# A hybrid attention/Fourier layer on eight cores: last token part of 128 with grouped scaling and stores, a fourth x slot, six rather than eight modulation blocks before attention and these later, head sums of squares on ScalarE, the second half of the first queries behind the Fourier part

## The chip, the cores and the metric

The kernel runs on all 8 cores of one Trainium2 chip. Each core works for itself: cores 2b and 2b+1 share batch entry b, each owns half of its 2048 tokens, computes keys and values for all of them, and does the queries, the output projection and the MLP for its own 1024. Nothing is exchanged between cores.

The time is the device time of the slowest core, in microseconds (us). A program on eight cores has a second, slower state in some executions: the cores of one die, or both, are granted a lower TensorE clock (in one execution of the kernel before four cores had 0.83 to 0.84 and the others 0.98, and it took 1936.8 us). Runs marked slow are left out everywhere; ratios use fast runs alone. "Clock" is the granted TensorE clock as a share of the full one.

Engines: PE is TensorE (PEld its weight loads), DVE is VectorE, ACT is ScalarE, POOL is GpSimd, SP is SyncE.

## The reference, cut to what matters

```python
h = modulate(rmsnorm(x, g1), sh1, sc1)
q, k, v, u = split_proj(h @ w_in)            # 12 query heads, 4 key/value heads, 4 Fourier groups
q = apply_axial_rope(rmsnorm(heads(q), q_g), tabs)
k = apply_axial_rope(rmsnorm(heads(k), k_g), tabs)
attn = latent_attention(q, k, v, kc, vc)     # over 256 context keys and 2048 latent keys
four = fourier_mix(u, w_f)
x = x + gt1 * (concat([attn, four]) @ w_out)
h2 = modulate(rmsnorm(x, g2), sh2, sc2)
x = x + gt2 * sq_relu_mlp(h2, w1, w2)
return rmsnorm(x, final_norm_g)
```

The six vectors `sh1 ... gt2` come from `silu(c) @ w_ada`. This matrix is read in 48 blocks of 1 MB (as bf16 on the chip). Blocks 8 to 15 (scale 1) are needed before the first projection, 0 to 7 (shift 1) soon after it, 16 to 47 only after attention.

## The kernel before: the parts that matter here

The program is first recorded as a list of operations with a priority ("level") each. A planner in the kernel file then orders the operations of every engine with a cost model, and adds the semaphore waits. Each operand is booked as one range of bytes:

```python
    def span(self, ap):                     # one range from the first to the last byte touched
        dims = list(ap.ap)
        row = dims[0][0]
        lo = hi = ap.offset % row
        ...
        return space, lo, hi
```

Loading x. Eighteen token tiles go through three slots of 8 KB per partition, from tile 6 on through two of them, because the third is reused for the "middle" modulation blocks (`wadm`, blocks 16 to 23):

```python
        ADM = [at('wadm', 160, [16, 256], BF16)]
        XS = [at('xs_%d' % i, 144 + 8 * i, [16, 128]) for i in range(3)]
        ...
            xi = n % 3 if n < 6 else n % 2
        ...
        first = [vu(n) for n in range(3)]            # three tiles before the first weights are complete
        ...
        for n in range(NLATE, 18):                   # NLATE = 7
            (some.pop(0) if some else vu(n))()()
            if n < NLATE + 5:
                chains[n - NLATE]()
            if n < NLATE + 8:
                ada(9 + n, ADM, 'adm', 1, 1, [4])    # eight blocks, from tile 7 on
```

Then the Fourier part, all eight tiles of the first four query heads (`q_block(0, ...)`), and attention, into which `side()` mixes the other query heads and modulation blocks 24 to 47.

The end. The last two blocks of the MLP are finished for tokens 0 to 511, then 512 to 767, then 768 to 1023. For each part and each of 16 row blocks: eight matmuls, a residual add on DVE, a square on ACT, a matmul with ones for the sum of squares; then the final norm:

```python
        for n, (tg, lo, hi) in enumerate(((0, 0, 512), (1, 0, 256), (1, 256, 512))):
            ...
            for d in range(16):
                a = ACC(tg, d)[:, lo:hi]
                if n == 2 and d % 3 == 1:
                    R.tt(a, a, rb, ALU.mult, eng='pool')
                else:
                    R.stt(a, a, fgc[:, d:d + 1], rp, ALU.mult, ALU.mult)
                R.dma('sp', rows(out_d, tg * 16 + d)[:, lo:hi], a, 'out%d' % (d % 4), load=False)
```

That is 48 stores, one for each row block and part.

Of the kernel before, what the change touches and what calls it, by code (L numbers as in the profile page):

```python
# [13 lines left out]
D = 2048  # L14
# [16 lines left out]
class Rec:  # L31
# [20 lines left out]
            a = a.rearrange("p (a b c) -> p a b c", a=shape[0], b=shape[1])  # L52
        return a

    def span(self, ap):
        dims = list(ap.ap)
        row = dims[0][0]
        lo = hi = ap.offset % row
        for step, n in dims[1:]:
            if step >= 0:  # L60
                hi += step * (n - 1)
            else:
                lo += step * (n - 1)
        es = 2 if ap.dtype == BF16 else 4
        space, b = self.base[ap.tensor.name]
        lo, hi = b + lo * es, b + (hi + 1) * es
        if space == 'P':
            lo, hi = lo // 2048 * 2048, -(-hi // 2048) * 2048
        return space, lo, hi


    def add(self, eng, fn, reads=(), writes=(), dur=0.1, dma=None, nbytes=0, level=None, after=()):
        r = [self.span(a) for a in reads]
        w = [self.span(a) for a in writes]
        i = len(self.ops)
        if dma is not None:
            self.dma_cnt[dma] = self.dma_cnt.get(dma, 0) + 16
            ev = ('d', dma, self.dma_cnt[dma])
        else:
            ev = ('c', eng, i)  # L80
        self.ops.append(dict(i=i, eng=eng, fn=fn, r=r, w=w, dur=dur, dma=dma, nbytes=nbytes, ev=ev, after=after,
                             prio=(self.level if level is None else level, i + self.lag)))
        return i
# [84 lines left out]
    def dma(self, q, out, in_, key, load=True, level=None, after=()):  # L168
        nb = 4 * 128 * (self.fs(out) if load else self.fs(in_))
        return self.add(q, lambda e: e.dma_start(out=out, in_=in_), [] if load else [in_], [out] if load else [],  # L170
                        0.55 if q == 'pool' else 0.06, dma=key, nbytes=nb, level=level, after=after)


    def graph(self):
# [228 lines left out]
KORDER = [ORDER[n] for n in (5, 6, 7, 0, 8, 1, 9, 2, 10, 3, 11, 4, 14, 15, 16, 17)]  # L403


CB = {}
CF = {}

# [17 lines left out]
def build_program():  # L426
# [25 lines left out]
    with ExitStack() as st:  # L452
# [58 lines left out]
        AD0 = [at('wada_%d' % i, 108 + 8 * i, [16, 256], BF16) for i in range(4)]  # L511
        ADM = [at('wadm', 160, [16, 256], BF16)]
        AD1 = [at('wadb_%d' % i, 144 + 8 * i, [16, 256], BF16) for i in range(3)]
        XS = [at('xs_%d' % i, 144 + 8 * i, [16, 128]) for i in range(3)]
        SQ = [at('sqx_%d' % i, 168 + 4 * i, [16, 128], BF16) for i in range(2)]
        Y = [at('y_%d' % i, 176 + 2 * i, [512]) for i in range(4)]
        YL = Y[0:1] + [at('yl_%d' % i, kb, [512]) for i, kb in enumerate((46, 54, 140, 142, 186, 190))]
# [112 lines left out]
        def evac(out, in_, which, n=2):  # L630
            R.copy(out, in_, 'act' if rot(which, n) == 0 else 'dve')

        def head_norm(y, slot):

            t2 = T2[slot]
            c = qst[:, rot('qst', 16), :]
            R.act(t2, y, AF.Square)
            R.add('dve', lambda e, a=c[:, 0:4], b=t2.rearrange("p (h d) -> p h d", h=4):
                  e.tensor_reduce(out=a, in_=b, axis=AX.X, op=ALU.add), [t2], [c[:, 0:4]], 0.6)
            R.act(c[:, 4:8], c[:, 0:4], AF.Ln, scale=1.0 / 128, bias=EPS)  # L640
            R.act(c[:, 8:12], c[:, 4:8], AF.Exp, scale=-0.5)
            return c[:, 8:12].unsqueeze(2).to_broadcast([128, 4, 128])
# [4 lines left out]
        def qk(bank, y, rstd, bias, rope, g2, dst, late=False, slot=None, on_act=False):  # L647
            if late:
                R.tt(y, y, bias, ALU.add)
            else:  # L650
                R.stt(y, PS[bank], rstd, bias, ALU.mult, ALU.add)
            s = rot('t12', 2) if slot is None else slot
            t1, t2, xb = T1[s], T2[s], XB[s]
            rh = head_norm(y, s)
            if rope is None:
                R.tt(h3(t1), h3(y), g2[:, 0:128].unsqueeze(1).to_broadcast([128, 4, 128]), ALU.mult)
            else:
                rog = ROG[rot('rope', 2)]
                four = lambda a: a.rearrange("p (c f n) -> p c f n", c=2, f=2)
                R.tt(four(rog), rope.rearrange("p (c n) -> p c n", c=2).unsqueeze(2).to_broadcast([128, 2, 2, 64]), four(g2), ALU.mult)  # L660
                cg, sg = rog[:, 0:128], rog[:, 128:256]
                R.tt(h3(t1), h3(y), cg.unsqueeze(1).to_broadcast([128, 4, 128]), ALU.mult)
                for f in range(2):
                    R.tt(h3(t2)[:, :, 64 * f:64 * f + 64], h3(y)[:, :, 64 - 64 * f:128 - 64 * f],
                         sg[:, 64 * f:64 * f + 64].unsqueeze(1).to_broadcast([128, 4, 64]), ALU.mult)
                R.tt(t1, t1, t2, ALU.add)
            if on_act:
                for i in range(4):
                    R.act(h3(xb)[:, i, :], h3(t1)[:, i, :], AF.Copy, scale=rh[:, i, 0:1])
            else:  # L670
                R.tt(h3(xb), h3(t1), rh, ALU.mult)
            return lambda tbank: qk_out(xb, dst, tbank)
# [10 lines left out]
        def vu(n):  # L683
            t = ORDER[n]
            R.level = 0.95
            r = 1 if t >= 16 else 0
            xi = n % 3 if n < 6 else n % 2
            x = XS[xi]
            R.dma('sp', x.rearrange("p k n -> p (k n)"), rows(xt_d, t), 'xs%d' % xi)
            sq = SQ[n % 2]  # L690
# [42 lines left out]
            def keys():  # L733
# [3 lines left out]
                if n < NLATE:  # L737
                    R.act(y, PS[b], AF.Copy, scale=rstd)

                def chain(slot=None):  # L740
                    R.level = 1
                    rope = None
                    if r == 0:
                        c = rot('ropek', 16)
                        assert ORDER[n] == KORDER[c]
                        rope = ROP[c // 2 % 2]
                        if c % 2 == 0:
                            R.dma('sp', rope.rearrange("p k n -> p (k n)"), rows(ropek_d, c // 2), 'rope%d' % (c // 2 % 2))
                        rope = rope[:, c % 2, :]
                    qk(b, y, rstd, BKC if r else BK, rope, kg2, kT[:, :, t * 128:(t + 1) * 128], n < NLATE, slot, True)(7 - rot('tb', 2))  # L750
                return chain
            return keys

        first = [vu(n) for n in range(3)]
        last = load_win(3, WK, 'wk', 0.1, last)
        for i in range(8):
            last = ada(i, AD0[0:2], 'adz', 0.2, 0.5, [7, 6], last)
# [5 lines left out]
        bias_bc(selb[0], 6, BV)  # L763
        bias_col(WU, 7, buc, cfv('dmask'))

        chains = [keys() for keys in first] + [vu(n)() for n in range(3, NLATE)]
        some = [vu(n) for n in range(NLATE, 10)]
        for n in (5, 6):
            chains[n](0)
        for n in range(NLATE, 18):  # L770
            if n >= 15:
                some += [vu(i) for i in range(15, 18) if n == 15]
            (some.pop(0) if some else vu(n))()()
            if n < NLATE + 5:
                chains[n - NLATE]()
            if n < NLATE + 8:
                ada(9 + n, ADM, 'adm', 1, 1, [4])


        def q_block(cbk, pbanks, tbanks):  # L780
            w = WQ[cbk % 2]
            bias_rows(w, tbanks[rot('tq', len(tbanks))], R.level)
            bq = BQ[cbk % 2]
            bias_bc(selb[0], tbanks[rot('tq', len(tbanks))], bq)
            for t in range(8):
                h, rstd = hslot[t]
                b = pbanks[rot('pq', len(pbanks))]
                R.acc(PS[b], [(h[:, k, :], w[:, k, :]) for k in range(16)])
# [51 lines left out]
        load_wq(0, 1.7)  # L840
        R.level = 1.8
        done = None
        for out in q_block(0, [0, 1, 2, 3, 4, 3, 4, 3], [5]):
            if done:
                done(5)
            done = out
# [8 lines left out]

        def side():

            q = [q_block(1, [6, 7], [7, 6]), q_block(2, [6, 7], [7, 6])]
            na, nq, done = 24, 0, None
            for u in range(24):  # L860
                while nq < 16 and nq < 1.2 * (u + 1):
                    if done:
                        done(6 + rot('tq', 2))
                    done = next(q[nq // 8])
                    nq += 1
                if nq == 16 and done:
                    done(6 + rot('tq', 2))
                    done = None
                yield
                while na < 48 and na - 24 < 1.1 * (u + 1):  # L870
                    prev[:] = ada(na, AD1, 'adb', 2, 2, [6, 7])
                    na += 1
                yield
# [115 lines left out]
                stage_a(NB - 1, j, tg)  # L989


        for n, (tg, lo, hi) in enumerate(((0, 0, 512), (1, 0, 256), (1, 256, 512))):
            for d in range(16):
                R.level = 4
                stage_b([NB - 2, NB - 1], d, tg, lo, hi)
# [1 line left out]
                a = ACC(tg, d)[:, lo:hi]  # L997
                R.act(sq, a, AF.Square)
                R.mms([(PS[n][:, lo:hi], ones, sq, d == 0, d == 15)])
                if n == 2 and d % 3 == 1:  # L1000
                    R.act(a, a, AF.Copy, scale=fgc[:, d:d + 1])
            R.level = 5
            rb = TN[n % 2][:, lo:hi]
            R.act(rb, PS[n][:, lo:hi], AF.Ln, scale=1.0 / D, bias=EPS)
            rp = rb
            if n == 2:
                rp = PS[n][:, lo:hi]
                R.act(rp, rb, AF.Exp, scale=-0.5)
            R.act(rb, rb, AF.Exp, scale=-0.5)
            for d in range(16):  # L1010
                a = ACC(tg, d)[:, lo:hi]
                if n == 2 and d % 3 == 1:
                    R.tt(a, a, rb, ALU.mult, eng='pool')
                else:
                    R.stt(a, a, fgc[:, d:d + 1], rp, ALU.mult, ALU.mult)
                R.dma('sp', rows(out_d, tg * 16 + d)[:, lo:hi], a, 'out%d' % (d % 4), load=False)
        R.emit(st)
    build_program.rec = R
    return nc
# [131 lines left out]
```

## Time and profile before

Median 1698.33 us of three runs (1697.06 to 1698.65). The first lines of the page of the slowest core: busy time by engine, then busy tenths in 40 slices, with the granted clock and the DMA share.

```profile
span 1696.6 us, 27987 instructions; the slowest of 8 cores (1683.6 to 1696.6 us)
PE 1599.2 (94%) x10582; PEld 813.1 (48%) x10582; DVE 714.9 (42%) x1288; ACT 618.0 (36%) x1253; POOL 61.4 (4%) x132
...
PE   2589998999999999999999999999999999999996
PEclk9689999999999999999999999999999999999998
DMA  9999877459475897036242355225532454235205
```

PE is full except in the first ten slices (42 us each) and the last. So look at the start by windows. The columns are PE, PEld, DVE, ACT and POOL busy time with instruction counts, the granted clock, the DMA share and GB/s.

```profile
core 2: us, PE busy (x) PEld busy (x) DVE busy (x) ACT busy (x) POOL busy (x), PEclk, DMA share, GB/s
0.00:120.00 120.00, 61.80 (x477) 27.25 (x478) 17.21 (x53) 21.29 (x33) 12.47 (x30) 0.83 1.00 191
120.00:240.00 120.00, 112.72 (x1094) 58.34 (x1093) 45.35 (x88) 73.35 (x177) 6.20 (x18) 0.96 0.90 200
240.00:320.00 80.00, 73.05 (x524) 35.71 (x523) 53.05 (x110) 43.24 (x131) 5.43 (x15) 0.98 0.79 131
320.00:420.00 100.00, 95.34 (x752) 52.24 (x751) 66.99 (x143) 46.23 (x106) 5.30 (x10) 0.98 0.63 106
```

Of the first 420 us PE is idle 77 us, 58 of them before 120 us, where the transfers are saturated. What PE waited for there (total us, times, longest):

```profile
PE ps L108 <- DMA wada_77<-w_ada: 22.9, 2, 22.5
PE ps L108 <- DMA wvu<-w_vu: 14.4, 7, 3.5
PE ps L108 <- DMA wada_78<-w_ada: 9.4, 3, 4.1
...
PE ps L108 <- DMA wadm<-w_ada: 4.2, 3, 2.8
PE ps L108 <- DVE h_62 L144: 3.2, 1, 3.2
PE ps L108 <- ACT sqx_88 L139: 3.2, 2, 2.5
PE ps L108 <- DMA wq_70<-w_in: 2.6, 1, 2.6
```

The end, from the timeline (columns: start, duration, engine, line) and from the instructions of the program's closing line (the q after an engine's name is its sequencer; each engine's program closes with a DRAIN):

```profile
1682.35 0.27 PE L108 MATMUL ps<-sqn_151,cb 128*128 128x256 bf16 x1 [0.71 <-ACT sqn_151 L139]
1684.23 3.46 POOL L144 TENSOR_TENSOR acc_146<-acc_146,tn_163 128x256 f32<-128x256 f32 x5 [94.04 <-ACT tn_163 L139]
1668.85 23.30 SPq L170 DMA_DIRECT2D out<-acc_146  x32
...
L380 POOLq DRAIN  x1: 12002/12002/12002, 1684.3 to 1684.3; - x1
L380 SPq DRAIN  x1: 7/7/7, 1693.8 to 1693.8; - x1
```

The last matmul ends 14 us before the span does.

### The profile page before, as it was taken

How to read it: one execution, taken by the hardware profiler on the slowest of the kernel's cores; microseconds unless marked ns; L12 is line 12 of the kernel's file. 1: busy time of each engine (PE TensorE's matmuls, PEld its weight loads, DVE VectorE, ACT ScalarE, POOL GpSimd, SP SyncE). 2: the span in 40 equal slices, each digit the busy share in tenths (PEclk: the TensorE clock that was granted, in tenths of full speed). 3: DMA queues.
4: the chain of work that ended last, by engine and by line, in shares of the span. 5: the costliest groups of instructions: out<-in, count | busy, mean ns of one | idle time of the engine just before them, and what ended most of it. 6: DMA issues, size and time to landing. Idle time of an engine off the chain costs nothing.

```text
span 1696.6 us, 27987 instructions; the slowest of 8 cores (1683.6 to 1696.6 us)
## 1 busy us (share of the span) xinstructions
PE 1599.2 (94%) x10582; PEld 813.1 (48%) x10582; DVE 714.9 (42%) x1288; ACT 618.0 (36%) x1253; POOL 61.4 (4%) x132
## 2 busy tenths in 40 slices
PE   2589998999999999999999999999999999999996
PEld 1234544446666766444444444444444444444455
DVE  1112286675465212243244444444444444444237
ACT  1045666236777897144211111111111111111233
POOL 1000000000000000000000000000000000000000
PEclk9689999999999999999999999999999999999998
DMA  9999877459475897036242355225532454235205
GB/s 196 172 212 216 198 151 130 79 91 164 87 124 97 173 180 187 1 72 128 50 93 38 69 99 100 50 51 100 100 68 45 87 100 87 39 74 100 50 7 193
DMA packets 27554, 180.45 MB, mean 106 GB/s; under 512 B 3104, under 2 KB 8480, under 8 KB 12064
## 3 DMA queue, kind: packets, MB, share of 16 engines
q0 software_dynamic: 14896, 140.68, 46.7%
q1 hardware_dynamic: 12528, 37.98, 7.0%
q8 instruction: 88, 1.44, 0.3%
q14 instruction: 42, 0.34, 0.1%
HBM read 310.94 MB, written 8.39 MB: 188 GB/s over the span
## 4 chain that ended last, share of the span: by engine, by line
PE 81%; DMA 15%; ACT 2%; issue 1%; DVE 1%; POOL 0%; DVEq 0%; ACTq 0%; POOLq 0%; SPq 0%
PE ps L108 80%; DMA wada_80<-w_ada 5%; DMA wadm<-w_ada 2%; DMA xs_87<-xt 2%; DMA xs_85<-xt 1%; DMA wada_78<-w_ada 1%; DMA wq_70<-w_in 1%; DMA wadb_82<-w_ada 1%; PE ps L120 1%; DMA wq_69<-w_in 1%; DVE acc_146 L147 1%; ACT h_2_149 L139 0%; ACT sqx_88 L139 0%; ACT h_63 L139 0%; ACT h_64 L139 0%
## 5 line engine op out<-in xcount | busy, mean ns | idle before, releaser
L147 DVE SCALAR_TENSOR_TENSOR acc_146<-ps,modcol,acc_146 128x512 f32<-128x512 f32 (+1 forms) x272 | 195.8, 720 | 256.5 <-PE ps L108 237.7
L108 PE MATMUL ps<-a_1_158,w_1_156 128*128 128x512 bf16 (+1 forms) x1088 | 238.2, 367 | 0.0
L108 PE MATMUL ps<-a_0_157,w_0_155 128*128 128x512 bf16 (+1 forms) x1088 | 238.1, 367 | 0.0
L147 DVE SCALAR_TENSOR_TENSOR acc_144<-ps,modcol,acc_144 128x512 f32<-128x512 f32 x128 | 96.2, 751 | 181.4 <-PE ps L108 172.0
L108 PEld LDWEIGHTS ps<-a_1_158,w_1_156 128*128 128x128 bf16 x1088 | 106.5, 98 | 114.6
L108 PEld LDWEIGHTS ps<-a_0_157,w_0_155 128*128 128x128 bf16 x1088 | 106.4, 98 | 113.4
L147 DVE SCALAR_TENSOR_TENSOR acc_145<-ps,modcol,acc_145 128x512 f32<-128x512 f32 x128 | 96.2, 751 | 140.4 <-PE ps L108 131.0
L108 PE MATMUL ps<-qT,kT 128*128 128x512 bf16 x432 | 153.8, 382 | 1.4 <-ACT pt_132 L139 0.5
L108 PE MATMUL ps<-h_0_147,w_0_153 128*128 128x512 bf16 x512 | 115.4, 379 | 0.0
L108 PE MATMUL ps<-h_0_147,w_1_154 128*128 128x512 bf16 x512 | 115.2, 379 | 0.0
L108 PE MATMUL ps<-h_2_149,w_0_153 128*128 128x512 bf16 x384 | 88.4, 379 | 1.1 <-ACT h_2_149 L139 1.1
L108 PE MATMUL ps<-h_2_149,w_1_154 128*128 128x512 bf16 x384 | 88.1, 379 | 0.0
L108 PEld LDWEIGHTS ps<-h_0_147,w_1_154 128*128 128x128 bf16 x512 | 50.2, 98 | 60.3
L108 PEld LDWEIGHTS ps<-h_0_147,w_0_153 128*128 128x128 bf16 x512 | 50.2, 98 | 60.2
L139 ACT ACTIVATE rs_162<-ps 128x512 f32<-128x512 f32 x32 | 19.1, 596 | 162.8 <-PE ps L108 162.8
L139 ACT ACTIVATE rs_161<-ps 128x512 f32<-128x512 f32 x32 | 19.1, 596 | 162.8 <-PE ps L108 162.8
L139 ACT ACTIVATE rs_159<-ps 128x512 f32<-128x512 f32 x32 | 19.1, 597 | 161.5 <-PE ps L108 161.5
L139 ACT ACTIVATE rs_160<-ps 128x512 f32<-128x512 f32 x32 | 19.1, 596 | 161.1 <-PE ps L108 161.1
L144 DVE TENSOR_TENSOR modcol<-ps,cf 128x4 f32<-128x4 f32 x48 | 7.5, 159 | 141.9 <-PE ps L108 141.9
L108 PEld LDWEIGHTS ps<-h_2_149,w_0_153 128*128 128x128 bf16 x384 | 37.3, 98 | 47.0 <-issue 2.1
L108 PEld LDWEIGHTS ps<-h_2_149,w_1_154 128*128 128x128 bf16 x384 | 37.5, 98 | 45.4
L108 PEld LDWEIGHTS ps<-qT,kT 128*128 128x128 bf16 x432 | 40.9, 98 | 19.7 <-issue 5.2
(404 smaller groups left out, 2307.2 us busy)
## 6 DMA issues: line engine op xcount, KB each, us to landing
w_0_155<-w POOLq DMA_DIRECT2D x8, 2048.0 KB, 22.5
w_1_156<-w POOLq DMA_DIRECT2D x8, 2048.0 KB, 22.2
w_0_153<-w POOLq DMA_DIRECT2D x8, 2048.0 KB, 15.7
w_1_154<-w POOLq DMA_DIRECT2D x8, 2048.0 KB, 15.9
xs_85<-xt SPq DMA_DIRECT2D x8, 1024.0 KB, 12.1
xs_86<-xt SPq DMA_DIRECT2D x8, 1024.0 KB, 11.3
wadm<-w_ada POOLq DMA_DIRECT2D x8, 1024.0 KB, 11.0
wadb_82<-w_ada POOLq DMA_DIRECT2D x8, 1024.0 KB, 14.4
```

Source lines behind the costliest of these rows:

```text
L108: ins = e.matmul(o, lhsT=l, rhs=r, start=a, stop=b)
L120: ins = e.transpose(out=o, in_=i_, identity=ident)
L139: self.add('act', lambda e: e.activation(out=out, in_=in_, func=func, scale=scale, **kw), reads, writes, dur, level=level)
L144: self.add(eng, lambda e: e.tensor_tensor(out=out, in0=a, in1=b, op=op), [a, b], [out], dur, level=level)
L147: self.add('dve', lambda e: e.scalar_tensor_tensor(out=out, in0=a, scalar=s, in1=b, op0=op0, op1=op1), [a, b] + ([] if isinstance(s, float ...
```

## The change

Its intent: take time off the end with a smaller last part, fewer and larger multiplies and stores; give PE a fourth tile early; move work off VectorE; and fill the wait for the next query weights with part of the first queries. The diff, cut to its core:

```diff
+CUT = 384
+LAST = [[(12, 4, 'pool', 1), (0, 4, 'dve', 2), (4, 4, 'dve', 2), (8, 4, 'dve', 2)],
+        [(12, 4, 'pool', 1), (0, 4, 'dve', 2), (9, 3, 'pool', 1), (4, 4, 'dve', 2), (8, 1, 'dve', 1)],
+        [(12, 4, 'pool', 2), (0, 4, 'dve', 4), (4, 4, 'dve', 4), (8, 4, 'dve', 4)]]
-        for n, (tg, lo, hi) in enumerate(((0, 0, 512), (1, 0, 256), (1, 256, 512))):
+        for n, (tg, lo, hi) in enumerate(((0, 0, 512), (1, 0, CUT), (1, CUT, 512))):
...
+                R.act(a, a, AF.Copy, scale=fgc[:, d:d + 1])         # every row block, on ScalarE
...
+            for d0, g, eng, step in LAST[n]:
+                for d in range(d0, d0 + g, step):
+                    a = grp(d, step)                                # step row blocks in one multiply
+                    R.tt(a, a, (rp if eng == 'dve' else rb).unsqueeze(1).to_broadcast([128, step, w]), ALU.mult, eng=eng)
+                R.dma('sp', out_d[...], grp(d0, g), 'out%d' % rot('out', 4), load=False)   # one store for g
```
```diff
-        XS = [at('xs_%d' % i, 144 + 8 * i, [16, 128]) for i in range(3)]
+        XS = [at('xs_%d' % i, kb, [16, 128]) for i, kb in enumerate((144, 152, 160, 192))]
+        XI = [0, 1, 2, 3, 0, 1, 2, 0, 1, 2, 0, 1, 0, 1, 0, 1, 0, 1]
-        first = [vu(n) for n in range(3)]
+        first = [vu(n) for n in range(4)]
...
-            if n < NLATE + 8:
-                ada(9 + n, ADM, 'adm', 1, 1, [4])
+            if 10 <= n < 16:
+                ada(6 + n, ADM, 'adm', 1, 1, [4], last)             # six blocks, later; two more in side()
...
+            if on_act:                                              # key heads
+                for i in range(4):
+                    R.act(h3(t2)[:, i, :], h3(y)[:, i, :], AF.Square, accum=c[:, i:i + 1])
...
-        for out in q_block(0, [0, 1, 2, 3, 4, 3, 4, 3], [5]):
+        for out in q_block(0, [0, 1, 2, 3], [5], range(4)):         # level 1.8
...
+        for out in q_block(0, [6, 7], [7, 6], range(4, 8)):         # level 1.9
```

Three parts are not in the short description. `span` became `spans`, which books a strided operand as several ranges (so that the key tiles of four heads no longer count as one large range); the planner's cost of a transfer issued by SP went from 0.06 to 0.45 us; and `side()` takes up the query tiles within attention a step later (`nq < 1.2 * u`, before `1.2 * (u + 1)`).

More of the change, by code (lines that the diff above doesn't have):

```diff
@@ L1 @@
 import heapq
+from itertools import chain
 import numpy as np
@@ L53, in buf, with spans @@
         return a
-    def span(self, ap):
+    def spans(self, ap):
         dims = list(ap.ap)
         row = dims[0][0]
-        lo = hi = ap.offset % row
-        for step, n in dims[1:]:
-            if step >= 0:
-                hi += step * (n - 1)
-            else:
-                lo += step * (n - 1)
         es = 2 if ap.dtype == BF16 else 4
         space, b = self.base[ap.tensor.name]
-        lo, hi = b + lo * es, b + (hi + 1) * es
-        if space == 'P':
-            lo, hi = lo // 2048 * 2048, -(-hi // 2048) * 2048
-        return space, lo, hi
+        off = ap.offset % row
+        lead = [0]
+        rest = dims[1:]
+        ext = 1 + sum(st * (n - 1) for st, n in rest[1:]) if len(rest) > 1 else 0
+        if len(rest) > 1 and rest[0][0] > ext and rest[0][1] <= 16 and space == 'S':
+            lead = [rest[0][0] * i for i in range(rest[0][1])]
+            rest = rest[1:]
+        out = []
+        for l in lead:
+            lo = off + l
+            hi = lo + sum(st * (n - 1) for st, n in rest)
+            x, y = b + lo * es, b + (hi + 1) * es
+            if space == 'P':
+                x, y = x // 2048 * 2048, -(-y // 2048) * 2048
+            out.append((space, x, y))
+        return out
     def add(self, eng, fn, reads=(), writes=(), dur=0.1, dma=None, nbytes=0, level=None, after=()):
-        r = [self.span(a) for a in reads]
-        w = [self.span(a) for a in writes]
+        r = [x for a in reads for x in self.spans(a)]
+        w = [x for a in writes for x in self.spans(a)]
         i = len(self.ops)
@@ L170, in dma @@
         return self.add(q, lambda e: e.dma_start(out=out, in_=in_), [] if load else [in_], [out] if load else [],
-                        0.55 if q == 'pool' else 0.06, dma=key, nbytes=nb, level=level, after=after)
+                        0.55 if q == 'pool' else 0.45, dma=key, nbytes=nb, level=level, after=after)
     def graph(self):
@@ L631, in evac, with head_norm @@
             R.copy(out, in_, 'act' if rot(which, n) == 0 else 'dve')
-        def head_norm(y, slot):
+        def head_norm(y, slot, on_act=False):
             t2 = T2[slot]
             c = qst[:, rot('qst', 16), :]
-            R.act(t2, y, AF.Square)
-            R.add('dve', lambda e, a=c[:, 0:4], b=t2.rearrange("p (h d) -> p h d", h=4):
+            if on_act:
+                for i in range(4):
+                    R.act(h3(t2)[:, i, :], h3(y)[:, i, :], AF.Square, accum=c[:, i:i + 1])
+            else:
+              R.act(t2, y, AF.Square)
+              R.add('dve', lambda e, a=c[:, 0:4], b=t2.rearrange("p (h d) -> p h d", h=4):
                   e.tensor_reduce(out=a, in_=b, axis=AX.X, op=ALU.add), [t2], [c[:, 0:4]], 0.6)
@@ L653, in qk @@
             t1, t2, xb = T1[s], T2[s], XB[s]
-            rh = head_norm(y, s)
+            rh = head_norm(y, s, on_act)
             if rope is None:
@@ L686, in vu @@
             r = 1 if t >= 16 else 0
-            xi = n % 3 if n < 6 else n % 2
+            xi = XI[n]
             x = XS[xi]
@@ L738, in keys, with link @@
                     R.act(y, PS[b], AF.Copy, scale=rstd)
-                def chain(slot=None):
+                def link(slot=None):
                     R.level = 1
@@ L750, in chain @@
                     qk(b, y, rstd, BKC if r else BK, rope, kg2, kT[:, :, t * 128:(t + 1) * 128], n < NLATE, slot, True)(7 - rot('tb', 2))
-                return chain
+                return link
             return keys
-        first = [vu(n) for n in range(3)]
+        first = [vu(n) for n in range(4)]
         last = load_win(3, WK, 'wk', 0.1, last)
@@ L764, in build_program @@
         bias_col(WU, 7, buc, cfv('dmask'))
-        chains = [keys() for keys in first] + [vu(n)() for n in range(3, NLATE)]
+        chains = [keys() for keys in first] + [vu(n)() for n in range(4, NLATE)]
         some = [vu(n) for n in range(NLATE, 10)]
@@ L775, in build_program, with q_block @@
                 chains[n - NLATE]()
-            if n < NLATE + 8:
-                ada(9 + n, ADM, 'adm', 1, 1, [4])
-        def q_block(cbk, pbanks, tbanks):
+            if 10 <= n < 16:
+                ada(6 + n, ADM, 'adm', 1, 1, [4], last)
+        def q_block(cbk, pbanks, tbanks, tiles=range(8)):
             w = WQ[cbk % 2]
-            bias_rows(w, tbanks[rot('tq', len(tbanks))], R.level)
             bq = BQ[cbk % 2]
-            bias_bc(selb[0], tbanks[rot('tq', len(tbanks))], bq)
-            for t in range(8):
+            if 0 in tiles:
+                bias_rows(w, tbanks[rot('tq', len(tbanks))], R.level)
+                bias_bc(selb[0], tbanks[rot('tq', len(tbanks))], bq)
+            for t in tiles:
                 h, rstd = hslot[t]
@@ L842, in build_program @@
         done = None
-        for out in q_block(0, [0, 1, 2, 3, 4, 3, 4, 3], [5]):
+        for out in q_block(0, [0, 1, 2, 3], [5], range(4)):
+            if done:
+                done(5)
+            done = out
+        done(5)
+        R.level = 1.9
+        done = None
+        for out in q_block(0, [6, 7], [7, 6], range(4, 8)):
             if done:
@@ L856, in side @@
         def side():
-            q = [q_block(1, [6, 7], [7, 6]), q_block(2, [6, 7], [7, 6])]
-            na, nq, done = 24, 0, None
+            q = chain(q_block(1, [6, 7], [7, 6]), q_block(2, [6, 7], [7, 6]))
+            na, nq, done = 22, 0, None
             for u in range(24):
-                while nq < 16 and nq < 1.2 * (u + 1):
+                while nq < 16 and nq < 1.2 * u:
                     if done:
                         done(6 + rot('tq', 2))
-                    done = next(q[nq // 8])
+                    done = next(q)
                     nq += 1
@@ L869, in side @@
                 yield
-                while na < 48 and na - 24 < 1.1 * (u + 1):
+                while na < 48 and na - 22 < 1.25 * u:
                     prev[:] = ada(na, AD1, 'adb', 2, 2, [6, 7])
@@ L989, in build_program @@
                 stage_a(NB - 1, j, tg)
-        for n, (tg, lo, hi) in enumerate(((0, 0, 512), (1, 0, 256), (1, 256, 512))):
+        for n, (tg, lo, hi) in enumerate(((0, 0, 512), (1, 0, CUT), (1, CUT, 512))):
+            w = hi - lo
             for d in range(16):
@@ L999, in build_program @@
                 R.mms([(PS[n][:, lo:hi], ones, sq, d == 0, d == 15)])
-                if n == 2 and d % 3 == 1:
-                    R.act(a, a, AF.Copy, scale=fgc[:, d:d + 1])
+                R.act(a, a, AF.Copy, scale=fgc[:, d:d + 1])
             R.level = 5
             rb = TN[n % 2][:, lo:hi]
-            R.act(rb, PS[n][:, lo:hi], AF.Ln, scale=1.0 / D, bias=EPS)
-            rp = rb
-            if n == 2:
-                rp = PS[n][:, lo:hi]
-                R.act(rp, rb, AF.Exp, scale=-0.5)
-            R.act(rb, rb, AF.Exp, scale=-0.5)
-            for d in range(16):
-                a = ACC(tg, d)[:, lo:hi]
-                if n == 2 and d % 3 == 1:
-                    R.tt(a, a, rb, ALU.mult, eng='pool')
-                else:
-                    R.stt(a, a, fgc[:, d:d + 1], rp, ALU.mult, ALU.mult)
-                R.dma('sp', rows(out_d, tg * 16 + d)[:, lo:hi], a, 'out%d' % (d % 4), load=False)
+            rp = PS[n][:, lo:hi]
+            R.act(rb, rp, AF.Ln, scale=1.0 / D, bias=EPS)
+            R.act(rp, rb, AF.Exp, scale=-0.5)
+            R.act(rb, rb, AF.Exp, scale=-0.5)
+            for d0, g, eng, step in LAST[n]:
+                grp = lambda d, m: (A1[:, d:d + m, lo:hi] if tg else A0[d // 8][:, d % 8:d % 8 + m, :])
+                for d in range(d0, d0 + g, step):
+                    a = grp(d, step)
+                    R.tt(a, a, (rp if eng == 'dve' else rb).unsqueeze(1).to_broadcast([128, step, w]), ALU.mult, eng=eng)
+                R.dma('sp', out_d[(tg * 16 + d0) * 128:(tg * 16 + d0 + g) * 128, lo:hi].rearrange("(g p) n -> p g n", p=128), grp(d0, g),
+                      'out%d' % rot('out', 4), load=False)
         R.emit(st)
```

## The prediction

> **What bounds the kernel.** Most of it is TensorE: the page gives PE 1599 of 1696.6 us busy. The windows table shows PE full from 400 us to 1676 us, with only 5 us of waits (PE waits). What can be saved is at the two ends.
>
> - Start, 0 to 420 us: PE is busy 343 us, idle 77. Of this 58 us lie before 120 us, where the DMA share is 0.9 to 1.0: PE waits on weight tiles of w_ada (22.9 us for the first ones), on w_vu (14.4 us), and at 100 to 108 us on WK and the fourth x tile (1.8 and 3.2 us). From 120 to 420 us only 19 us are idle: modulation weights 8.3, squares of x (late x tile) 3.2, the WQ loads 4.0, small ones.
> - End: the last matmul ends at 1682.6 us (timeline), the span 14 us later. In it are Ln/Exp (1 us), eleven multiplies on VectorE (4.4 us), five on GpSimd, and above all 128 KB stores that SyncE issues one by one at 0.73 us; the last is issued by 1692.15, 4.5 us before the end.
>
> **The change, costed.**
>
> 1. *End.* The last part has 128 columns, its multiplies are grouped by four (estimate 0.65 us each from 0.69 us for 128x512; three on VectorE beside two GpSimd ones of 0.7 us), with four stores in place of 16. From the last residual add to the end was 14.9 us; I estimate 8.5: 1.8 to the first multiply, 2 of multiplies, 0.7 issue, 4 to land. The 384-column part queues 3.1 MB of stores just before, at about 250 GB/s 12 us, which can add 1 to 2. The two parts should take PE as long as two of 256 (16 us each; 108 ns a matmul). The Trainium skill ("TensorE: Matmul & The Clock Gate", "Back-to-back issue gap") gives about 56 ns isolated but 81 ns sustained for 128 columns; no trace here shows which. At 81 ns, plus 0.7 us of ScalarE per output row block, the 128 part would take 11 us, not 8.5: 2 us lost. Net gain 3 to 6 us.
> 2. *Fourth x slot.* One more MB before the critical weights: at 185 GB/s the weight chain slips 5.7 us. In return PE has its fourth tile at once, and the third slot is kept until tile 9, so x comes further ahead. Net gain 2 to 4 us.
> 3. *Modulation blocks.* Two of them (11 us of transfer each) move from the saturated start into attention, where DMA is 0.36 to 0.86 busy. Gain 2 to 4 us.
> 4. *Head squares on ScalarE.* Takes 18 reductions of 0.68 us off VectorE, which is 80 to 96% busy at 220 to 280 us; adds about 0.9 us each to ScalarE (four 0.39 us instructions for one of 0.62), 16 us, which has room (58% at 220 to 320 us). Zero, within 2 us.
> 5. *Second half of the first queries behind Fourier.* WQ 1 starts to load earlier and PE has 14 us of work under it: gain 3 to 5 us of the waits at 357 to 397 us.
>
> Sum: about 14 us.
>
> **Predicted: 1684 us, range 1674 to 1693; faster by over 2% 0.04, within 2% 0.95, slower 0.01.**
>
> **Right if** the windows table to 420 us shows about 67 us of PE idle, not 77, no WQ wait near 357 us, and the last matmul is followed by 8 to 9 us. **Wrong if** ScalarE becomes what key tiles wait for at 220 to 300 us, if the late stores crowd the last ones, if the extra x tile delays the first weights by more than it gives back, or if the clock is granted lower.

## More of the kernel before

A POOL line that turned out to matter more than it looks: the timeline of POOL, which issues the weight loads in program order. `wadm` is a middle modulation block, `wq_69` the weights of the first queries. Columns: start, duration, engine, line.

```profile
131.32 0.53 POOL L170 DMA_DIRECT2D wadm<-w_ada  x1 [6.34 <-ACT h_64 L139]
199.26 0.53 POOL L170 DMA_DIRECT2D wadm<-w_ada  x1 [8.42 <-PE ps L108]
...
294.36 0.53 POOL L170 DMA_DIRECT2D wadm<-w_ada  x1 [6.38 <-PE ps L108]
300.39 0.53 POOL L170 DMA_DIRECT2D wq_69<-w_in  x1 [0.40 <-issue]
```

The first block is fetched at 131 us and its one slot is free again only at 199, when PE has used it; and the query weights stand in the queue behind the last one.

## The result, and the profile after

Median 1682.51 us of four runs (1681.68 to 1685.42), against 1698.49 us of four runs of before (1697.06 to 1699.38). The ratio is 0.991, 95% interval 0.9893 to 0.9927; it is the mean time of one kernel's fast runs over that of the other's of the same rounds, so not quite the ratio of these medians. The gain is 16 us where 14 were predicted.

The windows of the slowest core after, and what PE waited for in the first 420 us:

```profile
core 5: us, PE busy (x) PEld busy (x) DVE busy (x) ACT busy (x) POOL busy (x), PEclk, DMA share, GB/s
0.00:120.00 120.00, 66.38 (x510) 29.40 (x511) 18.78 (x56) 24.43 (x43) 12.62 (x39) 0.82 1.00 192
120.00:240.00 120.00, 115.92 (x1121) 59.89 (x1119) 52.05 (x104) 81.75 (x236) 5.26 (x10) 1.00 0.87 199
240.00:320.00 80.00, 75.35 (x512) 37.44 (x510) 47.90 (x96) 46.65 (x201) 4.01 (x13) 0.98 0.57 105
320.00:420.00 100.00, 98.29 (x853) 56.95 (x852) 62.21 (x140) 58.77 (x129) 5.83 (x11) 0.99 0.68 117
```
```profile
PE ps L116 <- DMA wada_77<-w_ada: 23.8, 3, 22.9
PE ps L116 <- DMA wvu<-w_vu: 21.9, 8, 5.2
PE ps L116 <- DMA wada_78<-w_ada: 5.0, 2, 4.0
PE ps L116 <- DMA wadm<-w_ada: 3.4, 1, 3.4
...
PE ps L116 <- DMA wq_69<-w_in: 0.9, 1, 0.9
```

The means over all eight cores say the same: PE busy in the first 420 us rose from 345.4 to 355.5 us, so 75 us idle became 65 (on the slowest cores, of which the prediction spoke, 77 became 64). The largest rise is at 120 to 240 us (111.6 to 116.5), where also the granted clock rose, from 0.961 to 0.995. An estimate: busy time times clock is 107 us before and 116 after, so 9 us more work is done in this stage, of which only 5 are less idle time. The other 3 to 4 us are clock, which the prediction did not count. The wait for `wvu` grew, since the fourth x tile is loaded among these weights (with three slots again, in u_xslot below, it falls back from 19.5 to 15.7 us, means of eight cores); the ones for late x tiles and query weights shrank.

One wait at 120 to 240 us all but went: the one for the last shift blocks (`wada`), 4.3 us before and 0.5 after in means of eight cores. On the slowest cores, first before, then after:

```profile
PE ps L108 <- DMA wada_78<-w_ada: 4.1, 1, 4.1
PE ps L116 <- DMA wada_77<-w_ada: 0.3, 1, 0.3
```

The POOL line after: the first `wadm` is fetched 44 us later, and the query weights 15 us earlier.

```profile
175.13 0.54 POOL L178 DMA_DIRECT2D wadm<-w_ada  x1
203.30 0.53 POOL L178 DMA_DIRECT2D wadm<-w_ada  x1 [27.63 <-PE ps L116]
...
285.06 0.53 POOL L178 DMA_DIRECT2D wq_69<-w_in  x1 [11.59 <-PE ps L116]
```

The end after:

```profile
1667.82 0.22 PE L116 MATMUL ps<-sqn_152,cb 128*128 128x128 bf16 x1 [0.56 <-ACT sqn_152 L147]
1669.78 1.41 POOL L152 TENSOR_TENSOR acc_147<-acc_147,tn_164 128x256 f32<-128x256 f32 x2
1664.29 11.44 SPq L178 DMA_DIRECT2D out<-acc_147  x9
...
L388 POOLq DRAIN  x1: 10446/10446/10446, 1669.4 to 1669.4; - x1
L388 SPq DRAIN  x1: 7/7/7, 1678.7 to 1678.7; - x1
```

From the end of the last matmul to the end of the span 12.0 us are left, not the 8 to 9 that I had predicted.

For the experiments I use one table of stages, each entry the mean over the eight cores of one profiled fast execution: start of the first attention matmul, start of the first sum-of-squares matmul of the final norm ("final norm"), start of the last matmul, end of the span. The time from the start of attention to the final norm depends on how many query tiles were done before attention, so the final norm is the place to compare.

| kernel | attention | final norm | last matmul | end | end minus last |
|---|---|---|---|---|---|
| before | 365.6 | 1614.9 | 1676.3 | 1690.6 | 14.2 |
| after | 338.0 | 1602.6 | 1663.4 | 1675.6 | 12.3 |

So 12.3 of the 15 us (in means) are there at the final norm, 0.6 come between it and the last matmul, 1.9 behind that.

### The profile page after: what moved, and what is told of

The parts are those of the page before. It is cut to its first block, busy times and chain, and to the rows that moved or that the text cites. A ratio compares the mean times of both kernels' runs of the same rounds, so it can differ in the third digit from the quotient of the medians.

```text
span 1680.1 us, 28006 instructions; the slowest of 8 cores (1671.1 to 1680.1 us)
## 1 busy us (share of the span) xinstructions
PE 1594.4 (95%) x10582; PEld 807.9 (48%) x10582; DVE 696.4 (41%) x1241; ACT 652.0 (39%) x1424; POOL 69.8 (4%) x140
## 4 chain that ended last, share of the span: by engine, by line
PE 83%; DMA 11%; ACT 3%; issue 1%; DVE 1%; POOL 1%; POOLq 0%; SPq 0%; ACTq 0%; DVEq 0%
PE ps L116 82%; DMA xs_86<-xt 4%; DMA wada_79<-w_ada 3%; DMA wvu<-w_vu 2%; DMA wadm<-w_ada 1%; DMA w_0_154<-w 1%; PE ps L128 1%; DMA wq_69<-w_in 1%; ACT sqx_90 L147 0%; ACT h_2_150 L147 0%; POOL acc_147 L152 0%; ACT h_64 L147 0%; ACT t_0_103 L147 0%; ACT sqx_89 L147 0%; ACT xb_105 L147 0%
## 5 line engine op out<-in xcount | busy, mean ns | idle before, releaser
L155 DVE SCALAR_TENSOR_TENSOR acc_147<-ps,modcol,acc_147 128x512 f32<-128x512 f32 (+2 forms) x272 | 194.4, 719 | 262.0 <-PE ps L116 245.1
L116 PE MATMUL ps<-a_1_159,w_1_157 128*128 128x512 bf16 (+2 forms) x1088 | 238.1, 366 | 0.0
L116 PE MATMUL ps<-a_0_158,w_0_156 128*128 128x512 bf16 (+2 forms) x1088 | 238.1, 366 | 0.0
L116 PEld LDWEIGHTS ps<-a_1_159,w_1_157 128*128 128x128 bf16 x1088 | 104.4, 98 | 117.5
L116 PEld LDWEIGHTS ps<-a_0_158,w_0_156 128*128 128x128 bf16 x1088 | 104.4, 98 | 116.1
L116 PEld LDWEIGHTS ps<-h_0_148,w_0_154 128*128 128x128 bf16 x512 | 50.1, 98 | 61.9 <-issue 1.8
L116 PEld LDWEIGHTS ps<-h_0_148,w_1_155 128*128 128x128 bf16 x512 | 50.2, 98 | 60.3
L116 PEld LDWEIGHTS ps<-h_2_150,w_0_154 128*128 128x128 bf16 x384 | 37.4, 98 | 47.1 <-issue 2.2
L116 PEld LDWEIGHTS ps<-h_2_150,w_1_155 128*128 128x128 bf16 x384 | 37.5, 98 | 45.3
```

The lines of the kernel that those rows point to most:

```text
L116: ins = e.matmul(o, lhsT=l, rhs=r, start=a, stop=b)
L155: self.add('dve', lambda e: e.scalar_tensor_tensor(out=out, in0=a, scalar=s, in1=b, op0=op0, op1=op1), [a, b] + ([] if isinstance(s, float ...
```

## The experiments

Names with u_ undo one part of the change, names with o_ do one part alone. They ran in three groups, each group on another chip. The kernel before had medians of 1698.1, 1695.95 and 1697.0 us (fast runs) on the three, so shifts of under 2 us between groups are not read.

| kernel | chip | fast runs (of) | median, fast | ratio to before, 95% | attention | final norm | last matmul | end | end minus last |
|---|---|---|---|---|---|---|---|---|---|
| c_after | A | 6 (6) | 1680.75 | 0.9892 (0.9862 to 0.9922) | 337.7 | 1601.2 | 1662.0 | 1674.3 | 12.3 |
| u_tail | A | 4 (6) | 1684.54 | 0.9938 (0.9878 to 0.9998) | 338.2 | 1600.6 | 1661.8 | 1676.0 | 14.2 |
| u_xslot | A | 4 (6) | 1685.48 | 0.9956 (0.9886 to 1.0025) | 343.1 | 1605.2 | 1666.2 | 1678.5 | 12.3 |
| u_head | A | 4 (6) | 1679.76 | 0.988 (0.9841 to 0.9918) | 351.8 | 1601.7 | 1662.5 | 1674.8 | 12.3 |
| u_qhalf | B | 4 (4) | 1679.40 | 0.9894 (0.9877 to 0.9912) | 352.1 | 1600.0 | 1660.7 | 1673.0 | 12.3 |
| u_ada | B | 5 (5) | 1685.75 | 0.9935 (0.992 to 0.995) | 335.8 | 1605.5 | 1666.3 | 1678.5 | 12.3 |
| u_spans | B | 2 (6) | 1675.78 | none given | 334.2 | 1597.7 | 1658.5 | 1670.8 | 12.3 |
| o_spans | B | 4 (5) | 1709.96 | 1.0076 (1.0058 to 1.0094) | 372.8 | 1622.8 | 1683.9 | 1698.1 | 14.2 |
| u_ada2 | C | 5 (5) | 1693.39 | 0.998 (0.9967 to 0.9993) | 366.2 | 1610.3 | 1671.1 | 1683.4 | 12.3 |
| o_ada | C | 3 (6) | 1705.79 | 1.006 (1.0037 to 1.0083) | 361.8 | 1615.8 | 1676.9 | 1691.1 | 14.2 |
| u_dur | C | 4 (6) | 1680.35 | 0.9902 (0.9884 to 0.9919) | 337.8 | 1600.7 | 1661.5 | 1673.8 | 12.3 |
| b_three | C | 4 (4) | 1673.11 | 0.9863 (0.9849 to 0.9877) | 347.2 | 1595.7 | 1656.9 | 1668.8 | 11.8 |

All gave correct results.

### c_after: the yardstick

No edit.

> The changed kernel again, unaltered, as the yardstick on this chip. Ratio to before 0.989 to 0.993 (about 15 us less), of which about 12 us are gained by the start of the MLP and 2 to 3 us from the first sum of squares of the final norm to the end.

Measured 0.9892, at the final norm 13.7 us ahead of before, 2.6 us more after it. As expected.

### u_tail: the end of before

```diff
-        for n, (tg, lo, hi) in enumerate(((0, 0, 512), (1, 0, CUT), (1, CUT, 512))):
+        for n, (tg, lo, hi) in enumerate(((0, 0, 512), (1, 0, 256), (1, 256, 512))):
...            # single multiplies and single stores, as before
```

> The changed kernel with the end of before (parts of 256, single stores). My theory after reading both traces: the end is worth only 2 to 3 us, because 4.2 MB of stores crowd behind the 384-column part; so 2 to 3 us slower than the changed kernel. Rival (the prediction): the end is worth 3 to 6 us. Time to the MLP unchanged within 1 us.

The final norm is unmoved (1600.6 against 1601.2), the time behind it grows by 2.3 us: 0.4 before the last matmul, 1.9 to 2.0 behind. The whole times are too scattered (fast runs 1682.44 to 1704.76), the stages are not. So the end is worth 2.3 us, below the 3 to 6 predicted. The size agrees with the theory; the reason did not, see b_three.

### u_xslot: three x slots again

```diff
-        XS = [... for i, kb in enumerate((144, 152, 160, 192))]
-        XI = [0, 1, 2, 3, 0, 1, 2, 0, 1, 2, 0, 1, 0, 1, 0, 1, 0, 1]
-        first = [vu(n) for n in range(4)]
+        XS = [... for i, kb in enumerate((144, 152, 160))]
+        XI = [0, 1, 2, 0, 1, 2, 0, 1, 0, 1, 0, 1, 0, 1, 0, 1, 0, 1]
+        first = [vu(n) for n in range(3)]
```

> The changed kernel with three x slots and three early tiles as before. Theory: the slot is worth 2 to 4 us, PE idles again at 100 to 108 us, and all of the loss is there at the start of the MLP. Rival: the extra megabyte before the first weights costs what it gives back, difference under 1 us, and the gain of the start comes from the moved modulation blocks and the moved queries.

The final norm comes 4.0 us later; the lower three of the fast runs are 1684.0 to 1685.67 against 1679.8 to 1684.38. On its slowest core PE again waits at 90 to 130 us for WK (2.3 us) and for the fourth tile (1.2 us), and 4.0 us for the squares of a late x tile at 190 to 240. The slot is worth the 2 to 4 us predicted, the rival falls.

### u_head: the head sums of squares as before

```diff
-            rh = head_norm(y, s, on_act)
+            rh = head_norm(y, s)
```

> The changed kernel with the head sums of squares by one square on ScalarE and a reduction on VectorE. Theory: no engine but TensorE binds at 220 to 320 us, so within 2 us of the changed kernel, either way. Rival: VectorE, 80 to 96 percent busy there before, held the key tiles back, and 3 us or more are lost.

The final norm moves by 0.5 us, the time not at all. VectorE is 8 us busier at 240 to 320 us (56.1 against 48.3, means of eight cores), ScalarE 6 us less (39.4 against 45.6), and nobody gains. In the changed kernel one head takes an activation of 0.30 us and a read of the accumulator of 0.19 us, and these overlap: one head starts 0.30 us after the other. The part is worth nothing here, as predicted.

### u_qhalf: all first queries before attention

```diff
-        for out in q_block(0, [0, 1, 2, 3], [5], range(4)): ...
-        for out in q_block(0, [6, 7], [7, 6], range(4, 8)): ...
+        for out in q_block(0, [0, 1, 2, 3, 4, 3, 4, 3], [5]): ...
```

> The changed kernel with all eight tiles of the first queries before attention, as before. Theory: 3 to 5 us slower than the changed kernel, with a wait on the next query weights again when the Fourier part ends. Rival: the scheduler fills the gap anyway, under 1.5 us.

Attention starts 14 us later and the final norm 1.2 us earlier, within the difference between chips. PE's waits for query weights are 1.1 us in all, against 0.9 in the changed kernel. So this part, for which I had predicted 3 to 5 us, is worth nothing: the 4.0 us of waits for query weights of before (slowest core) shrink to 1.1 without it. The first query weights are loaded earlier (285 instead of 300 us), and the next experiments show that this hangs on the modulation blocks.

### u_ada and u_ada2: the modulation blocks

u_ada puts the two moved blocks back, at the late start; u_ada2 undoes the start too.

```diff
 # u_ada
-            if 10 <= n < 16:
+            if 10 <= n < 18:
-            na, nq, done = 22, 0, None
+            na, nq, done = 24, 0, None
...            # and the pace of the blocks within attention to match
 # u_ada2: the same in side(), and
-            if 10 <= n < 16:
-                ada(6 + n, ADM, 'adm', 1, 1, [4], last)
+            if n < NLATE + 8:
+                ada(9 + n, ADM, 'adm', 1, 1, [4])
```

> The changed kernel with eight modulation blocks in the start rather than six. Theory: 22 us of transfer return to a stage where the DMA is busy, 2 to 4 us slower. Rival: those transfers only fill slack after 240 us, where the changed kernel's DMA share is 0.36 to 0.8, under 1 us.

> The changed kernel with the middle modulation blocks wholly as before: eight of them, from tile 7 on instead of tile 10, without the wait for the shift blocks. The earlier undoing kept the late start and cost 4.3 us up to the final norm. Theory: the late start is the part of the gain that is still missing, because before its loads stood between the shift blocks and the x tiles at 130 to 240 us; so 4 to 9 us more are lost, 8 to 13 us in all against the changed kernel, and TensorE's busy time at 120 to 240 us falls from 116.8 back to 112 to 114. Rival: the late start does nothing, 4 to 5 us in all.

u_ada loses 4.3 us at the final norm; its ratio is 0.9935 where the changed kernel has 0.9892. The two extra blocks are issued at 291.91 and 310.50 us, and what stands behind them in POOL's order, a small table of the Fourier part, is issued at 322.08 instead of 291.89, the second query weights at 351 instead of 338. So the loss is not in the saturated start, where I had looked for it: PE's busy time up to 240 us is that of the changed kernel (182.0 against 182.1 us, means of eight cores), and 3.4 us less from 240 to 420 us. The queue order at 290 to 350 us is the likely cause; the slowest core shows no single long wait there.

u_ada2 loses 9.1 us at the final norm, and its ratio (0.998) is within 0.2% of before: nearly the whole gain is gone, 12.6 us by the medians of two chips. PE is busy 112.8 us at 120 to 240 us (means of eight cores), not 116.8, as expected. Its slowest core, waits of the first 420 us and the POOL timeline:

```profile
PE ps L116 <- DMA wadm<-w_ada: 10.4, 2, 8.6
```
```profile
162.49 0.53 POOL L178 DMA_DIRECT2D wadm<-w_ada  x1 [7.77 <-ACT ua L147]
198.80 0.53 POOL L178 DMA_DIRECT2D wadm<-w_ada  x1 [22.68 <-PE ps L116]
...
304.62 0.53 POOL L178 DMA_DIRECT2D wq<-w_in  x1 [9.41 <-PE ps L116]
```

The first middle block is again fetched early and sits in its slot until 199 us, the eight loads follow each other through one slot, each waiting for PE to use the last, PE waits once 8.6 us for one, and the query weights come at 305 us. The granted clock at 240 to 320 us is 0.930 (0.972 in the changed kernel): a lower clock goes with these waits.

A second loss is as large. With the early start a middle block is loaded among the last shift blocks, and PE waits for these again: 4.4 us at 120 to 240 us (means of eight cores; u_ada 0.7, the changed kernel 0.4, before 4.3). The line of the slowest core:

```profile
PE ps L116 <- DMA wada<-w_ada: 5.2, 1, 5.2
```

The waits for `wadm` itself rise from 3.6 to 7.6 us (means, up to 420 us).

### o_ada: the modulation part alone

```diff
 # in the kernel before
-            if n < NLATE + 8:
-                ada(9 + n, ADM, 'adm', 1, 1, [4])
+            if 10 <= n < 16:
+                ada(6 + n, ADM, 'adm', 1, 1, [4], last)
-            na, nq, done = 24, 0, None
+            na, nq, done = 22, 0, None
-                while na < 48 and na - 24 < 1.1 * (u + 1):
+                while na < 48 and na - 22 < 1.25 * u:
```

> The kernel before with the modulation part alone (six middle blocks from tile 10, the rest in attention). Theory: 8 to 13 us faster than before, most of the gain of the change. Rival: without the fourth x slot x tiles bind, and it gives under 5 us.

It gains nothing: its final norm is at 1615.8 (before 1614.9), and its three fast runs (1703.1 to 1711.09) are slower than before. PE waits 5.8 us for the squares of a late x tile and 5.9 us for query weights. Here the x tiles still alternate between two slots from tile 6 on, so the slot that the later start frees stays empty; and the pace of the query tiles within attention was left as before. The slots alone can't be the reason: u_xslot has the same three slots in the same order, with the rest of the change, and is 9.7 us ahead of before at the final norm. So undoing this part costs most of the gain, yet alone it brings none. What else it needs (the pace of the query tiles, or another part by way of the planner's order) was not tested.

### u_spans, o_spans, u_dur: the parts not in the short description

```diff
 # u_spans: several ranges for the accumulators alone
-        if len(rest) > 1 and rest[0][0] > ext and rest[0][1] <= 16 and space == 'S':
+        if len(rest) > 1 and rest[0][0] > ext and rest[0][1] <= 16 and space == 'S' and ap.tensor.name.startswith('acc'):
 # o_spans: the new spans() in the kernel before, nothing else
 # u_dur
-                        0.55 if q == 'pool' else 0.45, dma=key, ...
+                        0.55 if q == 'pool' else 0.06, dma=key, ...
```

> The changed kernel where the finer bookkeeping of strided tiles serves the accumulators alone (the store part needs it to be free of races) and the key and query tiles are tracked as one range again. Theory: the first attention matmul has the same 2229 matmuls before it, so within 1.5 us. Rival: false waits between key or query tiles and attention return, and 3 us or more of the gain of the start are lost.

> The kernel before with the finer bookkeeping and nothing else. Theory: within 1.5 us of before. Rival: this unnamed part of the change gives 3 us or more by itself.

> The changed kernel with the build-time planner's cost of a SyncE transfer issue back at 0.06 us; it moves some instructions of the start, no work. Theory: within 2 us. Rival: the planner's order alone is worth 3 us or more, as the finer bookkeeping was (3.5 us lost in the changed kernel, 8 us in the one before).

Both theories about the bookkeeping fall. In the changed kernel the finer ranges cost 3.5 us at the final norm (1597.7 without them, two fast runs of 1674.99 and 1676.56; the other four were slow), and alone in the kernel before they cost 7.9 us at the final norm and 0.8% in all. They can only remove dependencies; what changes is the planner's order. In the changed kernel one wait has the size of the loss: PE stands 2.4 to 4.1 us, on each core, in front of a `wadm` block at 268 to 273 us. In u_spans the waits for `wadm` are gone (0.0 us up to 420 us against 3.5, means of eight cores). The changed kernel, then u_spans:

```profile
271.40 0.99 PE L116 MATMUL ps<-silu,wadm 128*128 128x2 bf16 x32 [3.38 <-DMA wadm<-w_ada]
265.46 0.94 PE L116 MATMUL ps<-silu,wadm 128*128 128x2 bf16 x32
```

In o_spans PE stands 5.9 us at 291 to 297 us in front of a `wadm` block that is not there yet, and behind it in its order stand 14 us of projection matmuls that run without a wait. u_dur moves a few instructions too, and is within 0.5 us.

### b_three: a try for a better one

```diff
 # u_spans and u_qhalf, and
-        for n, (tg, lo, hi) in enumerate(((0, 0, 512), (1, 0, CUT), (1, CUT, 512))):
+        for n, (tg, lo, hi) in enumerate(((0, 0, 512), (1, 0, 256), (1, 256, 384), (1, 384, 512))):
...            # LAST: the 256 part with 4 multiplies on POOL, both 128 parts as the last one was
```

> A try for a better one: changed kernel, coarse bookkeeping except for the accumulators, first queries whole before attention, and the second token half ended in parts of 256, 128 and 128. Up to the final norm 3 to 5 us less than the changed kernel (the sum of the two undoings, 3.5 and 1.2). For the end: if the stores are held by bytes that come after the 384 part (my theory), the time from last matmul to end falls from 12.3 to 8 to 9.5 us, and the last parts take 1 to 2 us longer on TensorE, net 1 to 3 us. Rival, SyncE's issuing holds the stores: with 12 rather than 9 issues nothing is gained there.

It beats both kernels: 1673.11 us, ratio 0.9863, 5 to 7 us less than the changed kernel (5.5 by the mean ends of the stage table, 6.6 when each median is set against before on its own chip). The gain is at the final norm, 5.5 us ahead of c_after, where the two undoings promised 4.7; from there to the end both take 73.1 us, so the third part brings nothing. On another chip, too, the kernel without the finer bookkeeping has no wait for `wadm` at 240 to 320 us.

At the end it is the most telling run. The stores do finish early: SP is through at 1667.0 us on the slowest core. But the span ends at 1671.9, and end minus last is 11.8 us, not 8 to 9.5. So neither my theory (bytes that come after the 384 part) nor the rival (SP's issuing) holds the end. The closing lines show what does:

```profile
1661.61 1.41 POOL L152 TENSOR_TENSOR acc<-acc,tn 128x256 f32<-128x256 f32 x2 [5.07 <-ACT tn L147]
...
L388 POOLq EVENT_SEMAPHORE  x2: 17/17/17, 1671.7 to 1671.8; - x2
L388 POOLq DRAIN  x1: 10062/10062/10062, 1661.6 to 1661.6; - x1
L388 SPq DRAIN  x1: 7/7/7, 1667.0 to 1667.0; - x1
```

POOL's closing DRAIN starts together with its last two multiplies (1661.6), lasts 10.06 us, and 0.23 us after its end the span ends. I then looked at the same lines on all eight cores of all fourteen kernels. Means over cores, in us:

| kernel | drain's length | drain's end minus end of POOL's last multiply | span's end minus drain's end | span's end minus end of the stores (SP) |
|---|---|---|---|---|
| before | 12.01 | 8.66 | 0.23 | 2.77 |
| u_tail | 12.00 | 8.66 | 0.23 | 2.63 |
| c_after | 10.47 | 8.66 | 0.23 | 1.23 |
| b_three | 10.06 | 8.66 | 0.23 | 4.85 |

The second column is 8.66 us, to 0.01, on every core of every kernel. The closing drains of PE, ACT and DVE end 0.04 to 0.05 us after their engine's last instruction, on every core too: only POOL's has this tail. The last column moves by 3.6 us between kernels, and the end does not follow it. The last multiplies of VectorE fit no better: on the slowest cores the drain ends 8.3 us after them before and 9.0 after the change. So the end hangs on POOL's last multiply and a drain that ends 8.66 us later. The gain of the end follows from that: POOL's last multiply ended 5.1 us after the last matmul before (1682.62 to 1687.69), 3.2 after the change (1668.04 to 1671.19), which is the 1.9 us measured. It has two multiplies there (1.41 us) instead of five (3.46 us).

Not run: a last part without multiplies on POOL, which would show whether the drain then ends early. If it did, the stores would hold the end, an estimated 1 us earlier in the changed kernel and 4.5 us in b_three (last column less about 0.3). What the drain waits for in these 8.66 us is also open.

## Why the prediction was right or wrong, point by point

The time was right: 1684 predicted (1674 to 1693), 1682.5 measured, "within 2%" as said. The idle time of the start was right too: 67 us predicted, 64 measured on the slowest core. The sum hides that its terms were not, and that 3 to 4 us of clock came on top.

1. **Fourth x slot** (2 to 4 us): 4.0 us. Right, for the reason given: the wait at 100 to 108 us goes, the wait for `wvu` grows.
2. **Modulation blocks** (2 to 4 us, two transfers taken out of a saturated stage): mis-sized. Undone as far as the number of blocks goes it is 4.3 us at the final norm; undone wholly, with the start from tile 7, 9.1 us there and 12.6 us in medians. I costed the bytes of two blocks and overlooked the order. The blocks go through one slot in POOL's program order, and everything behind them (the query weights, a table of the Fourier part) is issued only when PE has used each block in turn. The late start counts as much as the two blocks: it takes a middle block out from among the shift blocks, for which PE waited 4.3 us. And the part brings nothing alone (o_ada).
3. **Head squares** (zero, within 2): 0.5 us. Right.
4. **Second half of the first queries** (3 to 5 us): wrong, nothing could be seen (-1.2 us). The waits that it was to fill were gone once the query weights came 15 us earlier. I had counted one saving under two causes.
5. **The end** (3 to 6 us net; 8 to 9 us after the last matmul): size and mechanism wrong. It was worth 2.3 us, and 12.0 us are left after the last matmul. I took the stores for what ended last, because their issues were the last lines of the timeline; POOL's closing drain ended later in all kernels. Grouping the stores removed nothing from the critical path; what helped was that POOL had two multiplies left instead of five, so that its last one came 1.9 us sooner. That two parts of 384 and 128 columns cost PE no more than two of 256 was right, and the loss of up to 2 us that I allowed did not come: from the final norm to the last matmul it is 60.8 us, before 61.4.
6. **Not in the prediction at all**: the finer bookkeeping of strided tiles, which costs 3.5 us in the changed kernel. I looked at what it allows (fewer dependencies) and not at what the planner makes of it (a wait of 2.4 to 4.1 us for a `wadm` block).

The undoings sum up to 4.0 + 9.1 + 0.5 - 1.2 - 3.5 - 0.5 = 8.4 us at the final norm, where 12.3 to 13.7 were gained. The remaining 4 to 5 us were not settled: o_ada shows that parts need each other, and the later query tiles within attention were not undone in any run. That my total fitted is in part luck: too much for the queries and the end, too little for the modulation blocks.

## What to carry to other kernels

Before costing the end of a kernel, look at every engine's last line, the closing drains too, and ask which ends last; a long row of stores can be off the critical path. When several loads share one slot and one in-order queue, what counts is not only their bytes but what else is loading then, what stands behind them in the queue and who must free the slot. Where a planner orders the instructions, test each part of a change by undoing it: here a harmless-looking refinement of the dependencies was a loss, and leaving it out, with the first queries whole and the end in three parts, made up a further gain of 5 to 7 us.

## What the Trainium skill lacked or had wrong

- "VectorE: DVE Perf Modes", section "The DRAIN you can't avoid", knows two kinds: a flush after each VectorE instruction, and drains of a program's preamble and postamble, about 12 ns on all five engines. The drains in this program's closing line are one per engine; whether they are the second kind isn't shown, and 12 ns doesn't describe them. Those of PE, ACT and DVE end 35 to 54 ns after their engine's last instruction; that of POOL lasts 10.06 to 12.01 us, ends 8.66 us after its last tensor multiply on every core of fourteen kernels, and sets the end of the span; that of SP took 7 ns. I found no page that has the cost for GpSimd.
- "TensorE: Matmul & The Clock Gate", section "Back-to-back issue gap", gives two figures for 128 columns, about 56 ns isolated and 81 ns sustained with weight loads. In the last part of the changed kernel groups of four matmuls of 128x128, each with its own weights, start 0.22 us apart (1664.12, 1664.34, 1664.56), 55 ns each, and in b_three (core 6) a run of 24, with 24 weight loads, starts at 1641.28 and the next matmul behind it at 1642.62, 56 ns each: the isolated figure holds here, the sustained one does not.
- The same page, section "HAM oscillation — how this bites in real kernels", says that idle gaps of PE bring its clock down. The runs agree, if one looks at the longest gap and not at the busy time. At 240 to 320 us the longest gap of a core is 3.9 to 8.6 us in u_ada2 (mean clock 0.930), 3.6 to 5.9 in o_spans (0.929), 2.9 to 4.2 in c_after (0.972) and at most 2.3 in u_spans (1.000); before, with less busy time than c_after (74.6 against 75.6 us), has 1.1 to 3.4 and 0.992.
